# Attention keys turned once, with the two components of a head side by side, and spread over the partitions by the copies out of PSUM

## The chip, the cores and the metric

The kernel runs on one core of one Trainium2 chip, in one launch. The metric is device time in microseconds (us), the median of the runs of a kernel. The engines have these names: PE (TensorE; PEld is its weight load), DVE (VectorE), ACT (ScalarE), POOL (GpSimd) and SP (SyncE, which issues DMAs here).

## The reference

One layer of a hybrid diffusion step: a feed-forward half step, a token mixer, and a second feed-forward half step, on 512 latent tokens and 128 context tokens (640 in all) of width 1024. The mixer runs differential attention, an mLSTM scan in both directions and gates side by side. The change touches the attention, and of that the keys:

```python
def diff_attention(q, k, v, lam):
    ...
        s = jnp.einsum('bqhcd,bkhcd->bhcqk', qi.astype(jnp.float32), kf) * scale
        pr = jax.nn.softmax(s, axis=-1)
        w = pr[:, :, 0] - lam * pr[:, :, 1]
        return jnp.einsum('bhqk,bkhv->bqhv', w, vf)
```

There are 8 heads; `c` is one of two components of 64 features. Each component has scores of its own, and the second softmax is subtracted from the first. Latent queries see the 512 latent keys and 256 cached context keys; context queries see the 128 context keys. The result of each head is normalised over its 128 features.

## The kernel before, in words

**Products.** A product of fp32 numbers is made of rounded parts: each operand is split into a high part (the value rounded to the PE's fp32r format) and a low part (what the rounding left), and the products high x high, low x high and high x low are added in PSUM.

**Scores.** PE contracts over the partitions, so queries and keys of a component must lie with their features on the partitions, and a component has only 64. The kernel uses all 128: for the queries, `qT` holds in component `c` the high part on one half of the partitions and the low part on the other. For the keys, `kH[:, c, :]` holds the high part of component `c` *twice*, once on each half of the partitions, and `kL[:, c, :]` the low part twice. One matmul `qT` with `kH` then gives high x high and low x high at once, one with `kL` gives the rest. `kH` and `kL` are tiles of [128, 2, 896]: for each component the columns 0 to 511 are latent keys, 512 to 767 the cached ones, 768 to 895 the context keys.

**Where the duplicates come from, before.** `k_tok` holds the normalised keys of a pair of heads with tokens on the partitions. `pack_keys` (L1561) writes the high part of a head's keys to `kpk` [128, 5, 4, 64], each component twice side by side, with two ACT copies; `queries` (L1578) writes the low part to `kp2` (named `kp` in the profile) in the same way, with two DVE subtractions. `turn_features` (L1568) then transposes on PE, per token tile of 128 and component, a block of 128 x 128 (one component, doubled): 5 x 2 transposes into three PSUM tiles `ps_qkT` of two, two and one token tiles. Each PSUM tile goes out with one copy over all 128 partitions: to `kH` by DVE (L1593), to `kL` by ACT (L1595; ACT's operations all stand under its helper's line, L51). The same function turns the packed queries.

**Order of the work.** Eight heads follow one another (loop at L1961). Within a head there are five query tiles: `scores`, `soft` (exponentials on ACT), `mix` and the scaling on DVE, `turn` (PE transposes of the weights, `ps_wT`), `values` (`ps_o`). PE does other work between these steps: units of the mixer's projections (`Fill`, L1245), matmuls `ps_t<-wH,hH` and the like, for which ACT rounds a weight block to `wH` and DVE makes `wL`. The table `UNITS` (L1954) says how many units stand where. At the change from one head to the next the loop does `queries` of the next head, a unit, `values(4)` and `finish_norm` of the old head. Behind an even head there follow `keys(0)` (turns `kpk` to `kH`), one unit, `keys(1)` (turns `kp2` to `kL`) and one unit; behind an odd head, five units, with `keys(0)` and `keys(1)` behind the first and the second. Then the next head's `scores(0)` begins. `finish_norm` (L1658) scales the old head's result `ao` on DVE; `finish` (L1667) transposes it on PE (`ps_aT`), behind the unit that follows the next head's `scores(0)`.

PE's instructions keep the order of the program. The orders of ACT, DVE and SP are chosen by a tile scheduler at build time, except inside blocks marked `written()`; each engine then works through its own list in order. The PSUM tiles `ps_qkT`, `ps_t`, `ps_wT`, `ps_o` and `ps_aT` share a pool of five buffers; the scores `sc` have one tile of three banks.

Of the kernel before, what the change touches and what calls it, by code (L numbers as in the profile page):

```python
# [7 lines left out]
F32 = mybir.dt.float32  # L8
F32R = mybir.dt.float32r
BF16 = mybir.dt.bfloat16  # L10
AF = mybir.ActivationFunctionType
ALU = mybir.AluOpType
# [19 lines left out]
def tile_trunk(ctx: ExitStack, tc: tile.TileContext, a: dict):  # L32
    nc = tc.nc
    vec = nc.vector
    as_written = [False]

    def placed(ins):
        if as_written[0] is in_row:
            i = ins.ins
            if i.engine in in_row:  # L40
                tc.add_manual_dep(
                    i, in_row[i.engine].name, mybir.DependencyInfo(mybir.DependencyClass.NoSync, mybir.DependencyReason.DATA),
                    reason="written",
                )
            in_row[i.engine] = i
        elif as_written[0]:
            tc.keep_in_program_order(ins)
        return ins

    def act(*args, **kw):  # L50
        return placed(nc.scalar.activation(*args, **kw))  # L51

    def tt(eng, out, in0, in1, op):
        return placed(eng.tensor_tensor(out=out, in0=in0, in1=in1, op=op))  # L54
# [22 lines left out]
    def tr(*args, **kw):  # L77
        tc.keep_in_program_order(nc.tensor.transpose(*args, **kw))  # L78
# [23 lines left out]
    def load(pool, shape, src, **kw):  # L102
        t = pool.tile(shape, F32, **kw)
        dma(t, src)
        return t
# [725 lines left out]
    with ExitStack() as ph:  # L831
        fp = ph.enter_context(tc.tile_pool(name="ffn1", bufs=1))
        psum = Banks(ph.enter_context(tc.tile_pool(name="ps1", bufs=1, space=PSUM)))
# [507 lines left out]
    identr = gq_p.tile([128, 128], F32R, name="identr")  # L1341
# [7 lines left out]
    psum = att.enter_context(tc.tile_pool(name="ps2", bufs=5, space=PSUM))  # L1349
# [193 lines left out]
    class Head:  # L1543
# [17 lines left out]
        def pack_keys(self):  # L1561
            hs = slice(self.h * 128, (self.h + 1) * 128)
            kv = self.kv = k_tok[self.pr][:, :, hs].rearrange("p t (c d) -> p t c d", c=2)
            self.kpk = ap.tile([128, 5, 4, 64], F32R, tag="pk", name="kpk", bufs=2)
            for i in range(2):
                self.at_act = act(self.kpk[:, :, i::2, :], kv, AF.Copy)

        def turn_features(self, pk, dst, key, ev):  # L1568
            for i0, n in ((0, 2), (2, 2), (4, 1)):
                p = psum.tile([128, 2, 2, 128], F32R, tag="mm", name="ps_qkT")  # L1570
                for i in range(n):
                    flat = pk[:, i0 + i].rearrange("p s d -> p (s d)")
                    for c in range(2):
                        tr(p[:, c, i, :], flat[:, 128 * c : 128 * c + 128], identr)
                o = 768 if key and i0 == 4 else i0 * 128
                ev(dst[:, :, o : o + n * 128].rearrange("p c (i t) -> p c i t", i=n), p[:, :, :n, :].bitcast(F32))

        def queries(self):  # L1578
            self.qT = ap.tile([128, 2, T], F32R, tag="qT", name="qT")
            self.kH = ap.tile([128, 2, 896], F32R, tag="kH", name="kH")  # L1580
            self.kL = ap.tile([128, 2, 896], F32R, tag="kL", name="kL")
            self.ao = ap.tile([128, 5, 128], F32, tag="ao", name="ao")
            self.turn_features(self.qpk, self.qT, False, lambda o, i: act(o, i, AF.Copy))
            self.kp2 = ap.tile([128, 5, 4, 64], F32R, tag="pk", name="kp2", bufs=2)
            for i in range(2):
                self.at_vec = tt(vec, self.kp2[:, :, i::2, :], self.kv, self.kpk[:, :, i::2, :].bitcast(F32), ALU.subtract)
            ck = load(ap, [128, 2, 256], a["cache_kd"][:, self.hd], tag="asq", name="ck")
            act(self.kH[:, :, 512:768], ck, AF.Copy)
            tt(vec, self.kL[:, :, 512:768], ck, self.kH[:, :, 512:768].bitcast(F32), ALU.subtract)

        def keys(self, part):
            if part == 0:
                self.turn_features(self.kpk, self.kH, True, lambda o, i: vec.tensor_copy(o, i))  # L1593
            else:
                self.turn_features(self.kp2, self.kL, True, lambda o, i: act(o, i, AF.Copy))  # L1595

        def scores(self, qi):
            s = ps_s.tile([128, 1536], F32, tag="sc", name="sc")
# [325 lines left out]
    ap = att.enter_context(tc.tile_pool(name="att", bufs=1, reuse_waits="tile"))  # L1924
# [36 lines left out]
    for hd in range(8):  # L1961
        H = heads[hd]
        odd = hd % 2
        for qi in range(5):
            n = UNITS[hd][qi]
# [26 lines left out]
        n = UNITS[hd][-1]  # L1992
# [40 lines left out]
    psum = ml.enter_context(tc.tile_pool(name="ps3", bufs=8, space=PSUM, reuse_waits="tile"))  # L2033
# [238 lines left out]
    psum = Banks(ctx.enter_context(tc.tile_pool(name="ps4", bufs=1, space=PSUM, reuse_waits="tile")))  # L2272
# [58 lines left out]
    t = [in_pools["q"].tile([128, 1024], F32R, tag=f"q{i}", name="wo") for i in range(4)]  # L2331
# [234 lines left out]
```

## Time and profile before

| | |
|---|---|
| runs | 1815.12, 1815.26, 1816.54 us; median 1815.26 |
| the profiled execution | 1815.7 us, of which its span is 1813.9 |
| granted PE clock | 0.999 (mean over the span) |
| key transposes on PE | 160 (80 of `kpk`, 80 of `kp`), 670.5 to 1029.9 us |
| copies of keys out of PSUM | 24 on DVE (`kH`), 24 on ACT (`kL`) |
| attention heads, 655 to 1070 us | PE busy 409.85 of 415.00 us, DVE 273.37, ACT 229.28 |

The profile is of one execution. Rows of the time order read: start, length (us), engine, line, operation, out<-in, form of the tiles, count, and in brackets how long the engine was idle before it and what it was then released by. Matmuls are pipelined, so two may overlap in these rows and the distance from one start to the next is what one costs. Rows of a tile's groups read: operation, tiles, count: shortest/median/longest ns, first and last start, forms.

### The profile page before, as it was taken

Reading aid. Unit: us, or ns where it says so; the run is one execution under the profiler, and the core shown is the slowest. Engines: PE = TensorE matmul, PEld = TensorE weight load, DVE = VectorE, ACT = ScalarE, POOL = GpSimd, SP = SyncE. Lnnn points to the kernel's source line nnn. Section 1 sums busy time; section 2 is a strip of 40 time slices with the busy share of each in tenths; the row PEclk is TensorE's granted clock in tenths of the full one; section 3 lists DMA queues with packets and bytes.
Section 4 is the critical chain, followed back from the end, with each engine's and each line's share of the span. In section 5 each row is a group of like instructions: output and inputs, shape, how many; then the busy total and the mean of one; then the engine's idle time right before and its main releaser. Section 6 shows DMA issues by size and latency. Waiting matters only on the chain.

```text
span 1813.9 us, 30780 instructions
## 1 busy us (share of the span) xinstructions
PE 1785.6 (98%) x12550; PEld 1744.6 (96%) x12550; DVE 1349.6 (74%) x2178; ACT 910.8 (50%) x1588; POOL 39.2 (2%) x69
## 2 busy tenths in 40 slices
PE   8999999999999999999999999999999999999998
PEld 6999999999999999999999998899999999999998
DVE  6879987677888765858584557977767888897485
ACT  5654544333655445556564547674336545554432
POOL 0000000100000000000000000000000000000010
PEclk9999999999999999999999999999999999999999
DMA  8355566977245434221221124576642355557992
GB/s 326 111 198 171 186 236 221 350 227 266 83 139 181 160 131 143 78 69 63 69 69 55 68 81 163 182 257 218 221 171 80 134 173 185 203 180 274 353 311 80
DMA packets 132207, 311.36 MB, mean 172 GB/s; under 512 B 10017, under 2 KB 93217, under 8 KB 119009
## 3 DMA queue, kind: packets, MB, share of 16 engines
q1 hardware_dynamic: 121122, 265.22, 42.3%
q0 software_dynamic: 10256, 41.55, 7.1%
q8 instruction: 98, 1.61, 0.4%
q10 hardware_dynamic: 688, 2.63, 0.4%
q14 instruction: 43, 0.35, 0.1%
HBM read 240.49 MB, written 68.87 MB: 171 GB/s over the span
## 4 chain that ended last, share of the span: by engine, by line
PE 85%; DVE 7%; DMA 4%; ACT 2%; issue 1%; SPq 0%; DVEq 0%; ACTq 0%
PE ps_f L75 48%; PE ps_p L75 14%; PE ps_t L75 12%; PE sc L75 2%; PE ps_n L75 2%; PE ps_o L75 2%; DVE ww L54 2%; PE ps_u L75 1%; DMA raw_a<-in_w_ada_k 1%; PE ps_wT L78 1%; PE ps_qkT L78 1%; DMA raw<-in_w2b 1%; DVE junk L814 1%; DMA P<-nm_dram 1%; DVE mn L1617 1%
## 5 line engine op out<-in xcount | busy, mean ns | idle before, releaser
L75 PE MATMUL ps_f<-S,ww 128*128 128x320 f32 x2400 | 387.5, 310 | 5.2 <-DVE ww L54 1.9
L75 PEld LDWEIGHTS ps_f<-S,ww 128*128 128x128 f32 x2400 | 359.8, 188 | 9.6 <-DVE ww L54 6.5
L54 DVE TENSOR_TENSOR ww<-raw,ww 128x2048 fp32r<-128x2048 f32 (+1 forms) x73 | 163.9, 2246 | 74.3 <-ACT ww L51 74.2
L75 PE MATMUL ps_t<-wH,hH 128*128 128x256 f32 x640 | 185.7, 290 | 0.9 <-DVE x L57 0.9
L75 PE MATMUL ps_f<-hm,ww 128*128 128x320 f32 x1176 | 185.8, 309 | 0.1
L75 PE MATMUL ps_t<-wH,hL 128*128 128x256 f32 x640 | 181.6, 284 | 0.9 <-DVE hL L54 0.9
L75 PE MATMUL ps_t<-wL,hH 128*128 128x256 f32 x640 | 181.4, 283 | 0.0
L75 PEld LDWEIGHTS ps_f<-hm,ww 128*128 128x128 f32 x1176 | 175.7, 188 | 0.6 <-DVE ww L54 0.6
L51 ACT ACTIVATE ww<-raw 128x2048 fp32r<-128x2048 f32 (+1 forms) x73 | 136.9, 1875 | 60.3 <-DVE raw L54 33.0
L54 DVE TENSOR_TENSOR raw<-raw 128x1024 f32<-128x1024 f32 x186 | 161.0, 865 | 2.2
L75 PE MATMUL ps_f<-hm,wB 128*128 128x320 f32 x1008 | 161.5, 309 | 0.0
L75 PE MATMUL ps_p<-hH,wH 128*128 128x320 f32 x480 | 151.1, 315 | 0.7 <-ACT aT L51 0.7
L75 PEld LDWEIGHTS ps_f<-hm,wB 128*128 128x128 f32 x1008 | 151.3, 188 | 0.0
L75 PE MATMUL ps_p<-hH,wL 128*128 128x320 f32 x480 | 148.3, 309 | 0.0
L75 PE MATMUL ps_p<-hL,wH 128*128 128x320 f32 x480 | 148.3, 309 | 0.0
L51 ACT ACTIVATE u<-ps_f 128x320 f32<-128x320 f32 x129 | 55.8, 433 | 161.5 <-PE ps_f L75 159.7
L75 PEld LDWEIGHTS ps_t<-wH,hH 128*128 128x128 f32 x640 | 123.0, 192 | 1.5 <-ACT nsq L51 1.1
L75 PEld LDWEIGHTS ps_t<-wH,hL 128*128 128x128 f32 x640 | 122.9, 192 | 1.1 <-DVE hL L54 1.1
L75 PEld LDWEIGHTS ps_t<-wL,hH 128*128 128x128 f32 x640 | 123.1, 192 | 0.4
L1617 DVE TENSOR_REDUCE mn<-sc 128x2 f32<-128x1536 f32 (+1 forms) x40 | 59.5, 1489 | 56.0 <-PE sc L75 55.8
L54 DVE TENSOR_TENSOR wB<-raw,wB 128x1024 fp32r<-128x1024 f32 x64 | 78.1, 1221 | 26.7 <-ACT wB L51 26.7
L51 ACT ACTIVATE wH<-raw 128x2048 fp32r<-128x2048 f32 (+1 forms) x45 | 75.4, 1681 | 42.2 <-PE ps_p L75 35.5
(309 smaller groups left out, 3621.9 us busy)
## 6 DMA issues: line engine op xcount, KB each, us to landing
g_dram<-g SPq DMA_DIRECT2D x44, 640.0 KB, 7.6
raw_a<-in_w_ada_c POOLq DMA_DIRECT2D x35, 512.0 KB, 4.7
g_dram<-g SPq DMA_DIRECT2D x24, 480.0 KB, 8.1
raw<-in_w1b SPq DMA_DIRECT2D x11, 1024.0 KB, 4.9
raw<-in_w3b SPq DMA_DIRECT2D x11, 1024.0 KB, 6.3
raw<-in_w1a SPq DMA_DIRECT2D x10, 1024.0 KB, 4.9
raw<-in_w3a SPq DMA_DIRECT2D x10, 1024.0 KB, 6.2
hm<-g_dram SPq DMA_DIRECT2D x7, 1280.0 KB, 12.5
```

Source lines behind the costliest of these rows:

```text
L51: return placed(nc.scalar.activation(*args, **kw))
L54: return placed(eng.tensor_tensor(out=out, in0=in0, in1=in1, op=op))
L75: tc.keep_in_program_order(nc.tensor.matmul(*args, **kw))
L78: tc.keep_in_program_order(nc.tensor.transpose(*args, **kw))
L814: placed(vec.tensor_tensor_reduce(out=junk, in0=raw, in1=self.csil[:, v, :], op0=ALU.mult, op1=ALU.add, scale=1.0, scalar=0.0, accum_out=m ...
L1617: placed(vec.tensor_reduce(out=mn, in_=sv, axis=AX.X, op=ALU.min))
```

## The change

Keys are packed once: `kpk` and `kp2` are [128, 5, 2, 64], the two components side by side, with one ACT copy and one DVE subtraction. `turn_features` becomes two functions. `turn_queries` does for the queries what it did. `turn_keys` transposes each token tile once (component 0 comes to lie on partitions 0 to 63, component 1 on 64 to 127): five transposes into two PSUM tiles, of four and one token tiles. Out of PSUM each component is copied twice: by DVE to the partitions it lies on, by ACT to the other half, for `kH` and `kL` alike. These copies have 64 partitions and 512 or 128 columns.

```diff
-            self.kpk = ap.tile([128, 5, 4, 64], F32R, tag="pk", name="kpk", bufs=2)
-            for i in range(2):
-                self.at_act = act(self.kpk[:, :, i::2, :], kv, AF.Copy)
+            self.kpk = ap.tile([128, 5, 2, 64], F32R, tag="pk", name="kpk", bufs=2)
+            self.at_act = act(self.kpk, kv, AF.Copy)
...
+        def turn_keys(self, pk, dst):
+            for i0, n, o in ((0, 4, 0), (4, 1, 768)):
+                p = psum.tile([128, 4, 128], F32R, tag="mm", name="ps_qkT")
+                for i in range(n):
+                    tr(p[:, i, :], pk[:, i0 + i].rearrange("p c d -> p (c d)"), identr)
+                v = p.rearrange("p i t -> p (i t)")[:, : n * 128].bitcast(F32)
+                for c in range(2):
+                    own, other = slice(64 * c, 64 * c + 64), slice(64 - 64 * c, 128 - 64 * c)
+                    vec.tensor_copy(dst[own, c, o : o + n * 128], v[own])
+                    act(dst[other, c, o : o + n * 128], v[own], AF.Copy)
...
-            self.kp2 = ap.tile([128, 5, 4, 64], F32R, tag="pk", name="kp2", bufs=2)
-            for i in range(2):
-                self.at_vec = tt(vec, self.kp2[:, :, i::2, :], self.kv, self.kpk[:, :, i::2, :].bitcast(F32), ALU.subtract)
+            self.turn_queries()
+            self.kp2 = ap.tile([128, 5, 2, 64], F32R, tag="pk", name="kp2", bufs=2)
+            self.at_vec = tt(vec, self.kp2, self.kv, self.kpk.bitcast(F32), ALU.subtract)
...
-            if part == 0:
-                self.turn_features(self.kpk, self.kH, True, lambda o, i: vec.tensor_copy(o, i))
-            else:
-                self.turn_features(self.kp2, self.kL, True, lambda o, i: act(o, i, AF.Copy))
+            self.turn_keys(*((self.kpk, self.kH), (self.kp2, self.kL))[part])
```

PE's order is the same but for the transposes that are gone. The scheduler's orders of DVE and ACT change. Lines behind the edit are 7 higher in the changed kernel (`mn`, L1617 before, is L1624).

DVE between head 0 and head 1, before, from the last copies of `kH` to the first reduction over the scores of head 1 (`ass`, `rv`, `rt`, `ry`: small steps of norms; `ss`: sums of squares for the next pair of heads):

```order
L1593 CAST kH<-ps_qkT 128x2x128 [waits PE_49]
L1663 TENSOR_REDUCE ass<-asq 128x5 [waits Activation_49]
L63 TENSOR_SCALAR rv<-ass 128x5 [waits DVE_49]
L57 SCALAR_TENSOR_TENSOR rt<-ry 128x5 [waits Activation_49]
L54 TENSOR_TENSOR rt<-rt,rv 128x5 [waits DVE_49]
L57 SCALAR_TENSOR_TENSOR ry<-rt,ry 128x5 [waits DVE_49]
L54 TENSOR_TENSOR ao<-ao,ry 128x640 [waits DVE_49]
L54 TENSOR_TENSOR wL<-raw,wH 128x2048 [waits DMAHW5_49,PE_49,Activation_49]
L1475 TENSOR_REDUCE ss<-rope 128x20 [waits DMAHW4_49,DMAHW3_49,DMAHW6_49,DMAHW2_49,DMAHW7_49,DMAHW1_49,Activation_49]
L1617 TENSOR_REDUCE mn<-sc 128x2 [waits PE_49]
```

And in the changed kernel, from the first copies of `kL` on:

```order
L1586 CAST kL<-ps_qkT 64x512 [waits PE_49]
L1586 CAST kL<-ps_qkT 64x128 [waits PE_49]
L54 TENSOR_TENSOR wL<-raw,wH 128x2048 [waits DMAHW5_49,Activation_49]
L1475 TENSOR_REDUCE ss<-rope 128x20 [waits DMAHW4_49,DMAHW3_49,DMAHW6_49,DMAHW2_49,DMAHW7_49,DMAHW1_49,Activation_49]
L57 SCALAR_TENSOR_TENSOR rt<-ry 128x5 [waits Activation_49]
L1586 CAST kL<-ps_qkT 64x512 [waits Activation_49]
L1586 CAST kL<-ps_qkT 64x128 [waits Activation_49]
L63 TENSOR_SCALAR rv<-ss 128x20 [waits DVE_49]
L54 TENSOR_TENSOR rt<-rt,rv 128x5 [waits DVE_49]
L57 SCALAR_TENSOR_TENSOR ry<-rt,ry 128x5 [waits DVE_49]
L54 TENSOR_TENSOR ao<-ao,ry 128x640 [waits DVE_49]
```

The copies of component 0 stand ahead of `wL` and `ss`, those of component 1 (the second 64x512 and 64x128) behind them; each of these waits for ACT, whose copy of component 0 reads the same bank. `ao` stands behind `wL` and `ss` now.

DVE between head 2 and head 3, before, around the row that normalises `ao` and the reduction `mn` over head 3's first scores:

```order
L54 TENSOR_TENSOR rt<-rt,rv 128x5 [waits DVE_49]
L54 TENSOR_TENSOR k_tok<-k_tok,ry 128x1280 [waits DVE_49]
L57 SCALAR_TENSOR_TENSOR ry<-rt,ry 128x5 [waits DVE_49]
L54 TENSOR_TENSOR k_tok<-k_tok,g_kn 128x256 [waits DVE_49]
L54 TENSOR_TENSOR ao<-ao,ry 128x640 [waits DVE_49]
L1617 TENSOR_REDUCE mn<-sc 128x2 [waits PE_49]
L54 TENSOR_TENSOR rope<-rope,ropeBk 128x1024 [waits Activation_49]
L54 TENSOR_TENSOR k_tok<-k_tok,ropeAk 128x1024
```

And in the changed kernel (it reads the same between head 4 and head 5):

```order
L54 TENSOR_TENSOR k_tok<-k_tok,ry 128x1280 [waits DVE_49]
L54 TENSOR_TENSOR rt<-rt,rv 128x5 [waits DVE_49]
L1624 TENSOR_REDUCE mn<-sc 128x2 [waits PE_49]
L54 TENSOR_TENSOR k_tok<-k_tok,g_kn 128x256 [waits DVE_49]
L57 SCALAR_TENSOR_TENSOR ry<-rt,ry 128x5 [waits DVE_49]
L54 TENSOR_TENSOR rope<-rope,ropeBk 128x1024 [waits Activation_49]
L54 TENSOR_TENSOR k_tok<-k_tok,ropeAk 128x1024
L54 TENSOR_TENSOR ao<-ao,ry 128x640 [waits DVE_49]
```

`ao` was ahead of `mn`; it is behind `mn` and the two products with the rope tables.

DVE in head 0, in the changed kernel, around the last copies of `kL` (`Ml`, `fg`, `e`, `b` are the mLSTM's gates):

```order
L54 TENSOR_TENSOR mn<-Ml,bl 64x5 [waits DVE_49]
L54 TENSOR_TENSOR e<-u,Ml 64x640
L1586 CAST kL<-ps_qkT 64x512 [waits Activation_49]
L54 TENSOR_TENSOR b<-fg,b 64x640 [waits DVE_49]
L1586 CAST kL<-ps_qkT 64x128 [waits Activation_49]
```

Before, `e` and `b` stood next to each other there, and DVE had no copy of `kL`.

More of the change, by code (lines that the diff above doesn't have):

```diff
@@ L1563, in pack_keys, with turn_queries @@
             kv = self.kv = k_tok[self.pr][:, :, hs].rearrange("p t (c d) -> p t c d", c=2)
-            self.kpk = ap.tile([128, 5, 4, 64], F32R, tag="pk", name="kpk", bufs=2)
-            for i in range(2):
-                self.at_act = act(self.kpk[:, :, i::2, :], kv, AF.Copy)
-        def turn_features(self, pk, dst, key, ev):
+            self.kpk = ap.tile([128, 5, 2, 64], F32R, tag="pk", name="kpk", bufs=2)
+            self.at_act = act(self.kpk, kv, AF.Copy)
+        def turn_queries(self):
             for i0, n in ((0, 2), (2, 2), (4, 1)):
@@ L1571, in turn_features @@
                 for i in range(n):
-                    flat = pk[:, i0 + i].rearrange("p s d -> p (s d)")
+                    flat = self.qpk[:, i0 + i].rearrange("p s d -> p (s d)")
                     for c in range(2):
                         tr(p[:, c, i, :], flat[:, 128 * c : 128 * c + 128], identr)
-                o = 768 if key and i0 == 4 else i0 * 128
-                ev(dst[:, :, o : o + n * 128].rearrange("p c (i t) -> p c i t", i=n), p[:, :, :n, :].bitcast(F32))
+                o = slice(i0 * 128, (i0 + n) * 128)
+                act(self.qT[:, :, o].rearrange("p c (i t) -> p c i t", i=n), p[:, :, :n, :].bitcast(F32), AF.Copy)
+        def turn_keys(self, pk, dst):
[8 more added lines that the diff above has]
+                    act(dst[other, c, o : o + n * 128], v[own], AF.Copy)
         def queries(self):
@@ L1582, in queries @@
             self.ao = ap.tile([128, 5, 128], F32, tag="ao", name="ao")
-            self.turn_features(self.qpk, self.qT, False, lambda o, i: act(o, i, AF.Copy))
-            self.kp2 = ap.tile([128, 5, 4, 64], F32R, tag="pk", name="kp2", bufs=2)
-            for i in range(2):
-                self.at_vec = tt(vec, self.kp2[:, :, i::2, :], self.kv, self.kpk[:, :, i::2, :].bitcast(F32), ALU.subtract)
+            self.turn_queries()
+            self.kp2 = ap.tile([128, 5, 2, 64], F32R, tag="pk", name="kp2", bufs=2)
+            self.at_vec = tt(vec, self.kp2, self.kv, self.kpk.bitcast(F32), ALU.subtract)
             ck = load(ap, [128, 2, 256], a["cache_kd"][:, self.hd], tag="asq", name="ck")
```

## The prediction

> **What bounds the kernel now.** I read the page's busy times first, then the chain that ended last, then PE's waits in the stretch that holds the attention heads, then the groups of the tiles that the change touches, and last the order of time around the places where the order of DVE changes.
>
> From the page: the engines' busy times, and the chain by engine.
>
> ```profile
> span 1813.9 us, 30780 instructions
> PE 1785.6 (98%) x12550; PEld 1744.6 (96%) x12550; DVE 1349.6 (74%) x2178; ACT 910.8 (50%) x1588; POOL 39.2 (2%) x69
> PE 85%; DVE 7%; DMA 4%; ACT 2%; issue 1%; SPq 0%; DVEq 0%; ACTq 0%
> ```
>
> PE is busy for 98% of the span: what it no longer does is won, and each microsecond that it waits is lost. DVE has a quarter of the span free, ACT half, so their work is dear only where PE waits for one particular result. The answer on waits, PE alone, from 640 to 1080 us, names every wait that it lists there (total us, times, longest):
>
> ```profile
> PE ps_wT L78 <- DVE p L57: 3.0, 7, 0.8
> PE sc L75 <- ACT p L51: 1.6, 3, 0.9
> PE ps_p L75 <- ACT aT L51: 0.7, 1, 0.7
> PE ps_o L75 <- ACT wT L51: 0.5, 1, 0.5
> ```
>
> 5.8 us in all, none of them for a key copy or for the normalised `ao`. The way to read the change is therefore: PE's saving, less the waits that it makes.
>
> **The change part by part.** The groups of its tiles (ns least/median/most, first and last start, forms), and one group of key transposes in the order of time with the matmul behind it:
>
> ```profile
> L78 PE MATMUL ps_qkT<-identr,kpk x80: 222/251/305, 670.5 to 1025.5; 128*128 128x128 f32 x80
> L78 PE MATMUL ps_qkT<-identr,kp x80: 223/251/278, 677.1 to 1029.9; 128*128 128x128 f32 x80
> L1593 DVE CAST kH<-ps_qkT x24: 414/680/692, 673.8 to 1026.5; 128x512 fp32r<-128x512 f32 x16, 128x256 fp32r<-128x256 f32 x8
> L51 ACT ACTIVATE kL<-ps_qkT x24: 387/594/606, 677.6 to 1030.7; 128x512 fp32r<-128x512 f32 x16, 128x256 fp32r<-128x256 f32 x8
> L51 ACT ACTIVATE kpk<-k_tok x16: 720/732/742, 652.9 to 1013.5; 128x640 fp32r<-128x640 f32 x16
> L54 DVE TENSOR_TENSOR kp<-k_tok,kpk x16: 816/820/827, 664.9 to 1021.9; 128x640 fp32r<-128x640 f32 x16
> 781.33 0.97 PE L78 MATMUL ps_qkT<-identr,kpk 128*128 128x128 f32 x10
> 782.14 0.35 PE L75 MATMUL ps_t<-wH,hH 128*128 128x256 f32 x1
> ```
>
> *Transposes (removed).* A group of ten holds PE from 781.33 to 782.14, 0.81 us; I take 0.085 us for one, as the matmuls overlap (251 ns each, but a pitch of a third). 160 become 80: 10 x 0.085 = **0.85 us less per head, 6.8 us in eight heads**. This is on the path.
>
> *Pack and subtract (removed).* One ACT copy of 732 ns and one DVE subtraction of 820 ns less per head. Nothing on PE waits for either now, so alone they bring nothing; they pay for the copies.
>
> *Copies out of PSUM (added).* Three of them in a row on DVE:
>
> ```profile
> 728.25 1.62 DVE L1593 CAST kH<-ps_qkT 128x512 fp32r<-128x512 f32 x3
> ```
>
> They take 1.62 us together, less than 680 + 680 + 414 ns: one of 512 columns starts 0.60 us behind another (1.62 less the last one's 0.414, by two), and I give one of 128 columns a pitch of 0.20. Per head, kH took DVE 680 + 680 + 414 ns and kL took ACT 594 + 594 + 387. Now each of the two engines makes eight copies per head on 64 partitions, four of 512 columns and four of 128. No row has these shapes, so the price needs bounds. One end: a copy on 64 partitions costs what it costs on 128 (680 ns for 512 columns; 128 columns by the line through 680 and 414 ns come to 0.28 us). The other end: half of that. The nearest row is an operation on 64 partitions, beside the 820 ns of the 128-partition subtraction above, both of 640 columns:
>
> ```profile
> 683.06 0.81 DVE L54 TENSOR_TENSOR e<-u,Ml 64x640 f32<-64x640 f32 x1
> 683.79 0.81 DVE L54 TENSOR_TENSOR b<-fg,b 64x640 f32<-64x640 f32 x1
> ```
>
> Half the partitions takes the same time, so I take the full price: on DVE 4 x 0.68 + 4 x 0.28 - 1.77 - 0.82 = +1.25 us per head, and on ACT 4 x 0.59 + 4 x 0.28 - 1.57 - 0.73 = +1.2 us. With a quarter and a half of their span free this is no bound. What counts is the order: the copies of one bank take turns (DVE component 0, ACT component 0, DVE component 1, ACT component 1), so each `kL` bank is complete only after four copies in a row on two queues with other work in them, where before one queue held it.
>
> [...] No row of this trace shows two engines on one bank. [...]
>
> *Place 1, from head 0 to head 1.* In the new order DVE has, behind the copies of component 0 of `kL`, the low part of a weight (`wL`, 2.29 us) and the sum of squares `ss` of the next pair, and only then component 1. Before:
>
> ```profile
> 733.77 1.08 ACT L51 ACTIVATE kL<-ps_qkT 128x512 fp32r<-128x512 f32 x2
> 733.91 2.29 DVE L54 TENSOR_TENSOR wL<-raw,wH 128x2048 fp32r<-128x2048 f32 x1 [1.17 <-ACT wH L51]
> 735.25 0.40 PE L75 MATMUL sc<-kH,qT 128*128 128x512 f32 x1
> 736.06 0.28 PE L75 MATMUL sc<-kL,qT 128*128 128x256 f32 x1
> 736.12 1.48 DVE L1475 TENSOR_REDUCE ss<-rope 128x20 f32<-128x1280 f32 x1
> 736.64 0.28 PE L75 MATMUL ps_t<-wH,hH 128*128 128x256 f32 x1
> 737.51 1.75 DVE L1617 TENSOR_REDUCE mn<-sc 128x2 f32<-128x1536 f32 x1
> ```
>
> `wL` waits for ACT (1.17 us idle), so it and `ss` stay where they are and DVE is free at 737.51. A small operation (0.2) stands ahead of the copy, which runs from 737.7 to 738.4; ACT's copy follows to 739.0. The first score matmul that reads component 1 of `kL` stood at 736.06; it now starts at 739.05, and the unit behind the scores, 0.58 us later as before, at 739.6 instead of 736.64: **+3.0 us**, with the 0.85 saved already inside. Queued behind the waiting matmul is everything of PE; DVE goes on to `ao` and waits for the scores with `mn`.
>
> *Place 2, from head 2 to 3 and from head 4 to 5.* The row of DVE that normalises `ao` stood ahead of `mn`; now it stands behind `mn` and two products with the rope tables, and PE transposes `ao` behind the first unit after the scores. Before, at head 3:
>
> ```profile
> 834.44 0.18 DVE L57 SCALAR_TENSOR_TENSOR rt<-ry 128x20 f32<-128x20 f32 x1 [1.00 <-ACT ry L51]
> 835.09 1.49 DVE L54 TENSOR_TENSOR k_tok<-k_tok,ry 128x1280 f32<-128x1280 f32 x1
> 836.61 0.42 DVE L54 TENSOR_TENSOR k_tok<-k_tok,g_kn 128x256 f32<-128x256 f32 x1
> 836.96 0.82 DVE L54 TENSOR_TENSOR ao<-ao,ry 128x640 f32<-128x640 f32 x1
> 837.36 0.28 PE L75 MATMUL ps_t<-wH,hH 128*128 128x256 f32 x1
> 837.69 1.75 DVE L1617 TENSOR_REDUCE mn<-sc 128x2 f32<-128x1536 f32 x1
> 839.36 1.22 DVE L54 TENSOR_TENSOR rope<-rope,ropeBk 128x1024 f32<-128x1024 f32 x1
> 840.23 0.71 PE L78 MATMUL ps_aT<-ident,ao 128*128 128x128 f32 x5
> 840.49 1.22 DVE L54 TENSOR_TENSOR k_tok<-k_tok,ropeAk 128x1024 f32<-128x1024 f32 x1
> ```
>
> Now: DVE's longer copies (four of 0.60 and four of 0.20 less 1.6, +1.6 by pitch) are met by the missing subtraction (-0.74) and by the idle 1.00, so `k_tok` x `ry` starts as before, about 835.15. By the pitch of the rows (1.41, 0.2, 1.67, 0.46, 1.13, 1.14, each with the start of the next) it, the small `rt`, `mn`, the gain with the small `ry`, and the two rope products end at 841.15, and `ao` ends at 841.97. PE, 0.85 us early, comes to the transposes at 839.4: it waits 2.6 us, net **+1.8 us**. Head 5's order is the same and its rows stand alike, 94 us later: **+1.8** again. By full durations instead of pitches it would be +2.7 each.
>
> *Place 3, head 0.* DVE makes its copies between the gates' operations. Before:
>
> ```profile
> 683.77 0.40 PE L75 MATMUL sc<-kH,qT 128*128 128x512 f32 x1
> 684.58 0.28 PE L75 MATMUL sc<-kL,qT 128*128 128x256 f32 x1
> 685.16 0.28 PE L75 MATMUL ps_t<-wH,hH 128*128 128x256 f32 x1
> ```
>
> In the new order component 1 of `kL` comes between `e` and `b`, and `b` began at 683.79. Up to and with that copy DVE has 4 x 0.60 + 3 x 0.20 = 3.0 us of copies where 1.6 to 1.7 stood, so it ends at 685.1 and ACT's behind it at 685.8. PE's matmul of 684.58 starts there, and the unit at 686.4 instead of 685.16: **+1.2**, and +1.7 by full durations.
>
> *The other heads.* Heads 2, 4 and 7 get no new wait: odd handovers have three units between keys and scores. Each brings -0.85; head 6 about -0.6, for a wait of 0.25. The cover is a unit of projections, 2.9 us (837.36 to 840.23); without it a copy chain of four turns, 2 x 0.68 + 2 x 0.59 = 2.5 us, would stand bare.
>
> *Sum:* 1.2 + 3.0 + 1.8 + 1.8 - 3 x 0.85 - 0.6 = **+4.7 us**; by full durations 1.7 + 3.0 + 2.7 + 2.7 - 3.15 = +7.0. The profiled run took 1815.7 us (span 1813.9 and 1.8 around it), 0.4 above the median of 1815.26; so 1820.4 beside the profiled run and **1820.0** as a median.
>
> **The rivals.** *A wash:* the waits of heads 0 and 1 come, those for `ao` don't, because DVE runs further ahead than the pitches say: 1.2 + 3.0 - 5 x 0.85 - 0.6 = -0.65, 1814.6 us. For it: the idle second ahead of `rt`; against it: 2.6 us would have to go in each.
> *Cheap copies:* 64 partitions cost half. Then place 3 costs nothing (-0.1), place 1 +2.35, place 2 +1.4 each: -0.1 + 2.35 + 2.8 - 2.55 - 0.6 = +1.9, 1817.2 us. Against it are the two 64x640 rows.
> *The other side, faster:* the transposes decide. If each of the four waits stays under a unit's cover, PE just does 80 transposes less: -6.8 us, 1808.5. It decides from the point where the gross waits (2.1 + 3.9 + 2.6 + 2.6 = 11.2) fall under 6.8 in all. For it is PE at 98%; against it, the order puts 3.8 us of `wL` and `ss` before a copy that PE needs.
> *It doesn't do what it says:* excluded for the transposes, which the order shows halved.
>
> **How the numbers follow.** Forecast 0.58 (0.55 of it slower, 0.03 the same), wash 0.20 (0.01 faster, 0.19 same), cheap copies 0.12 (0.10 same, 0.02 slower), full gain 0.08, and 0.02 for longer waits than I counted. A measurement of this kernel can tell about 0.2%, 3.6 us, from no change, so slower begins at 1818.9 us and faster ends at 1811.6. Faster 0.09, same 0.32, slower 0.59. The likeliest case alone spans 1818.2 (one of the two `ao` waits missing, -1.8) to 1822.3 (full durations). The range goes from the wash, with a quarter of a microsecond for the spread of its runs, 1814.3, to 1823.5, full durations with one more wait of a place-3 size, and leaves out the full gain.
>
> **What would show it.** Right, if PE waits in the new profile for ACT `kL` ahead of `sc` in heads 0 and 1 (about 2 and 4 us) and for DVE `ao` ahead of `ps_aT` at heads 2 and 4 (about 2.6 each), with PE's busy time some 7 us lower and the 64x512 copies at about 0.68 and 0.59 us. It is wrong if these waits are under a microsecond, if the copies cost half, if waits elsewhere than at these four places grow by more than 2 us, or if the stretch behind attention, which the change doesn't touch, moves by more than 1 us.

## The result, and the profile after

The changed kernel takes 1825.85 us (median of 6 runs, 1823.74 to 1830.18) beside 1815.19 for the kernel before (6 runs, 1813.88 to 1816.54): a ratio of 1.0063, 95% interval 1.0053 to 1.0074. It is slower, as forecast, but by 10.7 us where 4.7 were forecast, and outside the range. The profiled execution took 1824.75 us, with a span of 1822.9.

The page's busy times and the chain by engine, after:

```profile
span 1822.9 us, 30699 instructions
PE 1783.2 (98%) x12470; PEld 1740.5 (95%) x12470; DVE 1360.5 (75%) x2210; ACT 921.0 (51%) x1620; POOL 39.4 (2%) x69
PE 79%; DVE 11%; DMA 5%; ACT 3%; issue 1%; SPq 1%; DVEq 0%; ACTq 0%
```

80 transposes are gone (12550 - 12470), and 6.8 us of busy time should have gone with them; PE's busy time fell by 2.4 only. Something made PE's other work longer. The waits of PE from 640 to 1090 us, after:

```profile
PE ps_aT L78 <- DVE rc L1638: 5.5, 2, 2.7
PE sc L75 <- ACT kL L51: 5.2, 3, 2.4
PE ps_wT L78 <- DVE p L57: 2.9, 6, 0.8
PE sc L75 <- ACT p L51: 1.6, 3, 0.9
PE ps_o L75 <- ACT wT L51: 0.5, 1, 0.5
```

The two rows on top are new, and they are the forecast's four waits: `ps_aT` twice (the row names `rc`, the small instruction right behind `ao` on DVE), and `sc` for `kL` once in head 0 and twice in head 1. The others are as before, but for the wait of `ps_p` for `aT`, 0.7 us, which is gone. At place 1, from head 0 to head 1, DVE's rows in the order of time read now:

```profile
731.42 0.88 DVE L1586 CAST kL<-ps_qkT 64x512 fp32r<-64x512 f32 x2 [0.43 <-PE ps_qkT L78]
733.70 2.29 DVE L54 TENSOR_TENSOR wL<-raw,wH 128x2048 fp32r<-128x2048 f32 x1 [1.40 <-ACT wH L51]
735.91 1.48 DVE L1475 TENSOR_REDUCE ss<-rope 128x20 f32<-128x1280 f32 x1
737.31 0.16 DVE L57 SCALAR_TENSOR_TENSOR rt<-ry 128x5 f32<-128x5 f32 x1
737.50 0.90 DVE L1586 CAST kL<-ps_qkT 64x512 fp32r<-64x512 f32 x2
```

Component 1 of `kL` stands behind `wL` and `ss`, at 737.50. ACT idles until DVE has copied, and PE until ACT has; ACT's row and PE's rows there:

```profile
738.23 0.76 ACT L51 ACTIVATE kL<-ps_qkT 64x512 fp32r<-64x512 f32 x2 [2.11 <-DVE kL L1586]
735.59 0.50 PE L75 MATMUL sc<-kL,qT 128*128 128x512 f32 x1 [0.96 <-ACT kL L51]
736.17 0.28 PE L75 MATMUL sc<-kH,qT 128*128 128x256 f32 x1
738.87 0.58 PE L75 MATMUL sc<-kL,qT 128*128 128x256 f32 x1 [2.42 <-ACT kL L51]
739.25 0.63 PE L75 MATMUL sc<-kH,qT 128*128 128x512 f32 x1
```

Two waits, 0.96 and 2.42 us. And a thing that was not forecast: the matmuls behind the wait are longer than those ahead of it (0.58 where one of 256 columns took 0.28, 0.63 where one of 512 took 0.40). The answer by windows shows why; its columns are the length, the busy times of PE, PEld, DVE, ACT and POOL, then the granted clock of PE and the DMA's share and rate. The windows begin and end where the clock changes, or a whole number of 3.413 us from there (the length is worked out below the rows):

```profile
735.03:738.44 3.41, 0.86 (x4) 0.60 (x4) 3.35 (x6) 1.27 (x4) 0.00 (x0) 1.00 0.38 86
738.44:741.86 3.42, 2.99 (x12) 2.79 (x13) 2.83 (x6) 0.88 (x4) 0.00 (x0) 0.50 0.52 220
741.86:745.27 3.41, 3.41 (x31) 3.41 (x31) 3.19 (x8) 3.13 (x7) 0.00 (x0) 1.00 0.00 0
...
840.84:844.25 3.41, 2.32 (x20) 2.11 (x18) 3.41 (x5) 2.60 (x6) 0.00 (x0) 1.00 0.11 38
844.25:847.67 3.42, 1.78 (x16) 1.81 (x17) 3.38 (x6) 1.21 (x3) 0.00 (x0) 1.00 0.00 0
...
939.83:943.24 3.41, 1.26 (x11) 1.29 (x12) 3.38 (x7) 1.37 (x5) 0.00 (x0) 1.00 0.06 20
943.24:946.66 3.42, 3.42 (x18) 3.42 (x17) 0.97 (x1) 0.35 (x2) 0.00 (x0) 0.50 0.25 96
```

Behind a window of 3.41 us in which PE was busy for 0.86 us only, the granted clock is 0.50 for just 3.42 us, and then 1.00 again. The same stands behind the wait for `ao` of head 5 (939.83: busy 1.26). Behind that of head 3, as long (2.73 us), it does not: there the wait lies across the border of two windows (busy 2.32 and 1.78), and leaves PE idle for 1.09 us of the one and 1.64 of the other. 943.24 lies 204.80 us behind 738.44, which is 60 times 3.413 us, and the third half-clock stretch of this trace, at 1127.56 behind attention, lies 184.32 us, 54 times 3.413, behind the second: in this trace the stretches start on a grid with steps of 3.413 us. The kernel before has one such stretch in attention, behind a window that was there to be read ahead of the prediction, and was not:

```profile
957.07:960.48 3.41, 1.73 (x13) 1.34 (x13) 2.01 (x6) 3.41 (x8) 0.00 (x0) 1.00 0.12 38
960.48:963.88 3.40, 3.40 (x18) 3.40 (x17) 2.27 (x6) 2.06 (x7) 0.00 (x0) 0.50 0.00 0
```

PE idles 1.68 us in that window, and not in one wait: it waits 0.90 us for `p` ahead of `sc` and 0.78 ahead of `ps_wT`, and the window's idle time is the sum. Here two short waits in one window stand ahead of a half-clock stretch, as one long wait does at 735.03.

**Where the time went.** I laid each matmul group of the one trace beside the same group of the other. Up to 655 us, ahead of everything that the change touches, the changed kernel's profiled execution was 1.7 us ahead (the runs differ there). At 1083 us, behind attention, it was 4.7 us late: attention lost 6.4 us. At 1260 it was 9.3 late, and it stayed so to the end: the stage behind attention lost another 4.5, up to 1.7 of them in the half clock at 1127 (half of 3.41 us, if PE has work for all of it).

### The profile page after: what moved, and what is told of

Read it like the earlier page. It is cut to its first block, busy times and chain, and to the rows that moved or that the text cites. A ratio compares the mean times of both kernels' runs of the same rounds, so it can differ in the third digit from the quotient of the medians.

```text
span 1822.9 us, 30699 instructions
## 1 busy us (share of the span) xinstructions
PE 1783.2 (98%) x12470; PEld 1740.5 (95%) x12470; DVE 1360.5 (75%) x2210; ACT 921.0 (51%) x1620; POOL 39.4 (2%) x69
## 4 chain that ended last, share of the span: by engine, by line
PE 79%; DVE 11%; DMA 5%; ACT 3%; issue 1%; SPq 1%; DVEq 0%; ACTq 0%
PE ps_f L75 46%; PE ps_p L75 14%; PE ps_t L75 9%; PE sc L75 2%; DVE ww L54 2%; PE ps_o L75 2%; DMA raw<-in_w2b 2%; PE ps_n L75 1%; DMA raw_a<-in_w_ada_k 1%; PE ps_wT L78 1%; DMA P<-nm_dram 1%; PE ps_u L75 1%; DVE junk L814 1%; DVE wL L54 1%; DVE mn L1624 1%
## 5 line engine op out<-in xcount | busy, mean ns | idle before, releaser
L1624 DVE TENSOR_REDUCE mn<-sc 128x2 f32<-128x1536 f32 (+1 forms) x40 | 59.6, 1489 | 54.5 <-PE sc L75 54.3
```

What stands on the lines that cost most here:

```text
L1624: placed(vec.tensor_reduce(out=mn, in_=sv, axis=AX.X, op=ALU.min))
```

## The experiments

Two theories stood against each other from the start, and a third came from the last sentence above. **A**: PE's saving of 6.8 us less the four waits, which come from the order on DVE, and (new) the half clock behind long waits. **B**: the doubled copies load DVE and ACT, and that makes everything a little longer. **C**: the stage behind attention loses its 4.5 us for a reason of its own. All ratios are to the kernel before on the same chip.

**The changed kernel again** (no edit).

> The changed kernel once more, for a second trace. Theory A (four waits of PE: component 1 of kL in heads 0 and 1, ao in heads 3 and 5; and, new, half the granted clock for some 3.4 us behind some of these waits, about 1.5 us each): the same four waits, 1.8 to 2.8 us each, and again half clock behind one to three of them, not always behind the same ones; 1823 to 1828 us. Theory B (the doubled copies load DVE and ACT, and everything gets a little longer): waits of PE spread over all heads. Theory C (the stage behind attention lost 4.5 us in the first trace for a reason of its own, an order of DMAs): that stage is again 4 to 5 us longer than before, whatever the clock does there.

1826.42 us (1823.17 to 1830.15; ratio 1.0060, 1.0047 to 1.0072; before 1815.63). The waits are the same to the tenth (5.5 and 5.2 us), at the same four places: A and not B. Half clock again behind the waits of head 1 and head 5, and not behind head 3's. But the stage behind attention, without a half-clock stretch, lost only 0.5 us in this trace. **C falls** as it was put, with 4 to 5 us each time. The length of that stage does vary, though: in the other traces of changed versions without a half clock there, it is 0.3 (covered_heads) to 3.4 us (one_engine) longer than in the first trace of before. Why was not tried.

**ao ahead of mn again, everything else as changed.**

```diff
             with written():
                 H.values(4)
-            H.finish_norm()
+                H.finish_norm()
```

> The changed kernel, with finish_norm in the written order, so that ao stands ahead of mn at heads 3 and 5; transposes and copies are as in the changed kernel. Theory A: the two waits of ps_aT for ao (2.7 us each) go, with the half clock behind one of them; at head 1 ao now stands ahead of component 1 of kL, which costs up to 0.8: 5 to 7 us less than the changed kernel, about 1819. Theory B: the copies are all there, so at most 1 us less, 1825. Theory C: the stage behind attention stays as long as in the changed kernel.

1819.53 us (1816.64 to 1822.47; ratio 1.0020, 1.0012 to 1.0029), 6.9 less than the changed kernel in the same comparison, with every copy still in place. PE's two largest waits:

```profile
PE sc L75 <- ACT kL L51: 5.7, 3, 2.9
PE ps_wT L78 <- DVE p L57: 3.0, 7, 0.8
```

The wait of `ps_aT` is gone from the list; that for `kL` is 0.5 longer, since `ao` now stands ahead of it in head 1. A wait of `ps_p` for `aT`, 0.7, is back (before has it too). The waits account for 5.5 - 0.5 - 0.7 = 4.3 us of the 6.9. The runs' mean clock (below) is 0.9964 where the changed kernel's is 0.9958, which gives about another 1. The rest, some 1.6, stays open; the six runs on the other side alone spread over 7.0. In this trace the wait of head 0 has half clock behind it: it is 1.80 us long and lies inside one window. In the changed kernel's first trace the same wait (1.79) lies across a border of the grid, which leaves PE idle for 1.31 us of one window and 0.47 of the next, and has none. The window of ao_early and the next:

```profile
684.07:687.48 3.41, 1.61 (x11) 1.32 (x10) 3.24 (x9) 2.06 (x5) 0.00 (x0) 1.00 0.53 153
687.48:690.90 3.42, 3.42 (x18) 3.42 (x17) 2.76 (x4) 2.20 (x5) 0.00 (x0) 0.50 0.40 142
```

**Each tile's copies on one engine**: as many copies, no turns.

```diff
-                    vec.tensor_copy(dst[own, c, o : o + n * 128], v[own])
-                    act(dst[other, c, o : o + n * 128], v[own], AF.Copy)
+                    for to in (own, other):
+                        if dst is self.kH:
+                            vec.tensor_copy(dst[to, c, o : o + n * 128], v[own])
+                        else:
+                            act(dst[to, c, o : o + n * 128], v[own], AF.Copy)
```

> The changed kernel, but each tile's copies are on one engine: DVE makes both halves of kH, ACT both halves of kL; as many copies of the same sizes, and no turns between engines. In its order DVE has no kL copy, and ao stands behind mn but ahead of the rope products. Theory A: the waits for kL at heads 0 and 1 go (5.2 us and the half clock behind), and those for ao fall to some tenths: the transposes' 6.8 us show, 1808 to 1811. Theory B: the same number of copies costs as before, 1822 to 1826. Theory C: the stage behind attention stays 4 us longer, so 1812 to 1815.

1822.1 us (1819.15 to 1824.34; ratio 1.0033, 1.0021 to 1.0045): missed by 11 us. The waits for `kL` did go, but others came:

```profile
PE ps_aT L78 <- DVE ao L54: 3.8, 2, 1.9
PE sc L75 <- ACT p L51: 3.0, 4, 1.4
PE ps_wT L78 <- DVE p L57: 2.7, 6, 0.8
PE ps_aT L78 <- DVE r L57: 2.0, 1, 2.0
PE ps_o L75 <- ACT wT L51: 0.5, 1, 0.5
PE sc L75 <- ACT kL L51: 0.4, 1, 0.4
```

Of 5.2 us for `kL` 0.4 are left: without turns there is no wait for the keys. I had taken `ao` right behind `mn` to be early enough; it came 1.9 us late at heads 3 and 5, and in head 1, where it now stood behind `wL`, `mn` and `ss`, 2.0 late (the row that names `r`). Behind head 3's, which leaves PE busy for 1.62 us in the window from 842.49, the next window is at 1.00; the mean clock of the five runs is 0.9956.

**The same with ao ahead of mn** (both edits).

> As one_engine, and finish_norm in the written order, so that ao stands ahead of mn at heads 3 and 5. Theory A: all four waits gone, 1808 to 1810, at most 1 us from one_engine. Theory B: 1822 to 1826. Theory C: 1812 to 1815.

1814.34 us (1811.98 to 1816.24; ratio 0.9993, 0.9984 to 1.0001): no difference from before that could be measured. All four waits are gone, as A has it, and 7.8 us with them, but 1808 to 1810 was expected, and that is missed by 4. By the shift of the matmuls attention gains 1.5 us where the transposes give 6.9: about 1.7 are lost in head 0, 0.5 in head 1 and 2 each at heads 3 and 5, and 0.8 of these come back. `sc` waits 3.0 for `p` (1.6 before) and `ps_wT` 4.2 (3.0). What `mn` gives is later there, behind ACT's copies in the one place and behind `ao` in the others; that this is the reason was not tried.

**Work for PE inside the waits.** The matmuls and transposes put in write where a later product starts anew; no result uses them.

```diff
                         mm(o, qT[:, c, qs], kH[:, c, k0:k1], start=True, stop=False)
+                        if qi == 0 and k0 == 0:
+                            for _ in range({(0, 1): 6, (1, 0): 4, (1, 1): 9}.get((self.hd, c), 0)):
+                                mm(s[:, 1024:1536], qT[:, 0, qs], kH[:, 0, 0:512], start=True, stop=True)
                         mm(o, qT[:, c, qs], kL[:, c, k0:k1], start=False, stop=True)
...
                 p = psum.tile([128, 4, 128], F32, tag="mm", name="ps_aT")
+                if i0 == 0 and self.hd in (2, 4):
+                    for _ in range(16):
+                        tr(p[:, 0, :], ident, ident)
```

> The changed kernel with matmuls that no result uses put into its four waits (6 before component 1 of kL in head 0, 4 and 9 before kL in head 1, each of 512 columns, written where a later product starts anew; 16 transposes of the identity before ps_aT of heads 2 and 4): PE is busy for most of each wait, and goes on when it did. The traces so far put half the granted clock, for 3.41 us, behind windows of 3.41 us in which PE idled for 1.7 to 1.9 us or more. Theory A with this clock: the waits stay as long, counted from the end of the work before them, but the half clock behind them goes; 1.5 to 1.7 us each, 2 to 3 of them in a run: 1821 to 1823.5, against 1826 of the changed kernel. Without an effect of the clock: 1826, or more where the fill is too long.

1820.66 us (1819.31 to 1822.31; ratio 1.0033, 1.0022 to 1.0044), 6.0 over the kernel before of the same comparison, where the changed kernel is 10.7 and 10.8 over its own: 4.7 less, by *adding* work. The trace has no half-clock stretch at all, so the place of the grid isn't known in it; around head 1's waits:

```profile
735.00:738.40 3.40, 3.38 (x21) 2.74 (x21) 2.80 (x2) 2.96 (x6) 0.00 (x0) 1.00 0.00 0
738.40:741.80 3.40, 3.03 (x15) 2.25 (x14) 3.24 (x10) 1.09 (x4) 0.00 (x0) 1.00 0.77 270
```

The useful matmuls start as late as in the changed kernel: beside the first trace of before, PE loses 2.9 us ahead of head 3's `ps_aT` in both. Only the clock behind is different. From 655 to 1083 us this trace loses 3.4 us where the changed kernel's lost 6.4 with two half-clock stretches, so one of them costs 1.5 us.

Each run lists its mean granted clock too: 0.9958 over the 12 runs of the changed kernel, 0.9993 over these 7, and 0.9988 over 71 runs of the kernel before. A half-clock stretch of 3.41 us takes 3.41 x 0.5 / 1820 = 0.00094 off that mean, so by estimate the changed kernel had 4.5 of them in a run, this one 0.7, before 1.3. By this estimate the clock cost the changed kernel (4.5 - 1.3) x 1.5 us = **4.8 us**; at 1.7 each, half of 3.41 us, it would be 5.4.

**One copy per tile over all partitions.** The copy writes the same block for both components, so the scores are not the reference's; half the transposes, as changed.

```diff
-                for c in range(2):
-                    ...
+                v = v[:, None, :].to_broadcast([128, 2, n * 128])
+                if dst is self.kH:
+                    vec.tensor_copy(dst[:, :, o : o + n * 128], v)
+                else:
+                    act(dst[:, :, o : o + n * 128], v, AF.Copy)
```

> Half the transposes as in the changed kernel, but one copy per PSUM tile over all 128 partitions, which writes the same block for both components (DVE for kH, ACT for kL, as before); the partitions' spreading is left out, so the scores are not those of the reference. In its order DVE stands as in before, with ao ahead of mn. Theory A: the transposes' 6.8 us show, no wait is added: 1807.5 to 1809.5. Were the transposes hidden by other work on PE or the saving given back elsewhere: 1813 to 1816.

1810.26 us (1807.44 to 1813.42; ratio 0.9972, 0.9961 to 0.9983), 4.4 less than before's 1814.62, where 5 to 7 were expected. Aligned with the first trace, PE gains 0.43 us at every one of the 16 groups, 6.9 in all; one wait came (`ps_aT` for `ao` in head 1, 1.5 us). The saving is real and on the path. About 1 us of it didn't reach the end; in this trace the stage behind attention was 2.1 longer.

**The changed way only where it is covered.**

```diff
+    NEW = (2, 4, 6, 7)
...
-            self.turn_keys(*((self.kpk, self.kH), (self.kp2, self.kL))[part])
+            if self.hd in NEW:
+                self.turn_keys(*((self.kpk, self.kH), (self.kp2, self.kL))[part])
+            else:
+                ...
```

(The dots stand for the lines of before; `pack_keys` and `queries` are split alike.)

> The changed way for heads 2, 4, 6 and 7 alone, the way of before for heads 0, 1, 3 and 5, where the changed kernel had its four waits. In its order ao stands ahead of mn at heads 3 and 5, and wL and ss behind the kH copies at head 1, as in before. Theory A: four heads bring 0.85 each, none adds more than 0.25: 1812 to 1812.6, faster than both. Were the doubled copies to cost something by themselves (theory B): half of the changed kernel's loss, 1820.

1811.57 us (1809.21 to 1814.42; ratio 0.9984, 0.9975 to 0.9992): half a microsecond under the forecast, and faster than both kernels. The list of PE's waits has the rows of before and no other:

```profile
PE ps_wT L78 <- DVE p L57: 2.7, 6, 0.8
PE sc L75 <- ACT p L51: 1.6, 3, 0.9
PE ps_p L75 <- ACT aT L51: 0.9, 1, 0.9
PE ps_o L75 <- ACT wT L51: 0.5, 1, 0.5
```

By the shift of the matmuls attention gains 3.5 us with all the doubled copies of four heads in it, where four times 0.85 is 3.4. So the copies cost nothing by themselves where the handover is covered: **B falls**.

**The kernel before again.**

> The kernel before, once more, for a second trace: waits in the heads as in the first (5.8 us in all), half the clock at another place or not at all, and the stage behind attention within 2 us of the first trace's length.

1814.46 us. The waits of PE in the heads are the same four rows as before, to the tenth. The half clock stands at 35.72 us and not at 960, so a run of before has it by chance as well; the stage from 1083 to 1260 us was within 0.2 us of the first trace's.

**One of the four waits alone, and filled.** Head 1 is added to the covered heads, then the fill of its waits.

```diff
-    NEW = (2, 4, 6, 7)
+    NEW = (1, 2, 4, 6, 7)
```

> covered_heads, with head 1 the changed way as well, in the changed kernel's order at that place (wL and ss ahead of component 1 of kL): one of the four waits alone. Theory A with the clock: the two waits for kL come back there (1.0 and 2.4 us, less the 0.85 of the transposes) and half the clock for one window behind them, sometimes two (1.5 to 1.7 us each): 4 to 5 us over covered_heads, 1815.5 to 1817. Waits without the clock: 2.5 over it, 1814.

> head1_alone with the fill of 4 and 9 matmuls, which no result uses, in its two waits. Theory A with the clock: PE goes on when it did, the half clock goes: 1.5 to 2 us under head1_alone, 2.5 over covered_heads, 1814. Without an effect of the clock: as head1_alone.

1815.93 us (1812.77 to 1818.38; ratio 1.0004, 0.9995 to 1.0013) and 1815.28 (1811.19 to 1822.15; 1.0005, 0.9995 to 1.0015). Head 1 alone costs 3.9 us (0.8 over before, where covered_heads is 3.1 under): the waits (0.96 + 2.43 in its trace, less 0.85) and some clock. The pair's difference, 0.65, is less than either interval is wide: the times neither show nor exclude the clock. The traces do show it, in the same windows of the one and of the other:

```profile
736.69:740.10 3.41, 0.98 (x6) 0.72 (x5) 3.28 (x8) 1.09 (x4) 0.00 (x0) 1.00 0.68 233
740.10:743.50 3.40, 3.40 (x17) 3.35 (x16) 3.30 (x6) 1.28 (x3) 0.00 (x0) 0.50 0.18 75
...
736.69:740.10 3.41, 3.02 (x14) 2.27 (x15) 3.28 (x9) 1.27 (x5) 0.00 (x0) 1.00 0.57 156
740.10:743.50 3.40, 3.40 (x27) 3.30 (x28) 3.30 (x6) 1.06 (x3) 0.00 (x0) 1.00 0.36 152
```

From 655 to 1083 us the filled trace is 1.5 us better, and that is this stretch. The runs' mean clocks differ by 0.0004 only, which is 0.4 of a stretch with a standard error as large, so how often it comes with head 1 alone is open.

**Six heads.** `NEW = (2, 3, 4, 5, 6, 7)`, and `finish_norm` in the written order behind heads 2 and 4.

> The changed way for heads 2 to 7, with ao in the written order behind heads 2 and 4 so that it stands ahead of mn, and the way of before for heads 0 and 1. Theory A: heads 3 and 5 bring 0.85 each, less some 0.3 to 0.5 for a later p in ao_early's trace: 0.6 to 1.2 us under covered_heads, 1810.4 to 1811. If short handovers lose their saving to later results whatever the order: as covered_heads or up to 1 us above it.

1812.41 us (1809.75 to 1815.66; ratio 0.9984, 0.9975 to 0.9993): as covered_heads, within the interval, and not the 1810.4 to 1811 of theory A. At heads 3 and 5 PE loses 0.7 us ahead of `ps_wT`, which waits for a later `p`, and gets 0.3 to 0.4 of it back; that takes a good part of what the transposes give there.

## Why the prediction was wrong

*The transposes.* 0.85 us per head, 6.8 in all: right (0.43 per group in one_wide_copy, by 16). Head 6 brought 0.6, as forecast.

*The copies' price.* Full price for half the partitions: right. The group of DVE's copies after, least, median and most, mixes 512 and 128 columns:

```profile
L1586 DVE CAST kL<-ps_qkT x32: 272/490/696, 680.3 to 1038.4; 64x512 fp32r<-64x512 f32 x16, 64x128 fp32r<-64x128 f32 x16
L51 ACT ACTIVATE kL<-ps_qkT x32: 256/432/597, 681.0 to 1038.8; 64x512 fp32r<-64x512 f32 x16, 64x128 fp32r<-64x128 f32 x16
```

The ends are the two forms: 0.27 and 0.70 us on DVE, 0.26 and 0.60 on ACT, where 0.28 and 0.68, 0.28 and 0.59 were taken. That they are no bound was right too (covered_heads).

*The four waits.* Right in place and cause, and near in length. Place 1: 0.96 + 2.42 = 3.4 us gross, and between the same matmuls of the two traces +2.95 net up to the last wait, forecast 3.0. Place 2, at head 3:

```profile
840.57 1.76 DVE L1624 TENSOR_REDUCE mn<-sc 128x2 f32<-128x1536 f32 x1
842.65 1.22 DVE L54 TENSOR_TENSOR rope<-rope,ropeBk 128x1024 f32<-128x1024 f32 x1
843.79 1.22 DVE L54 TENSOR_TENSOR k_tok<-k_tok,ropeAk 128x1024 f32<-128x1024 f32 x1
844.93 0.82 DVE L54 TENSOR_TENSOR ao<-ao,ry 128x640 f32<-128x640 f32 x1
845.89 0.74 PE L78 MATMUL ps_aT<-ident,ao 128*128 128x128 f32 x5 [2.73 <-DVE rc L1638]
```

`ao` stands behind `mn` and the rope products and ends at 845.75, and PE waits 2.73 us for it; 2.74 at head 5; 2.6 forecast. Place 3: 1.79 gross, 2.1 forecast.

*The sum.* Attention lost 6.4 us in the first trace. Taking out its two half-clock stretches there (1.5 each), and the one that before's trace had there and this one lacked (1.5), leaves 6.4 - 3.0 + 1.5 = 4.9, against +4.7. filled_waits, which has these waits without the half clock, comes to the same: 3.4 + 1.5 = 4.9. As far as waits and transposes go, the sum was right, and in part by luck: net of the transposes and the clock, heads 0, 1, 3 and 5 cost 1.5 + 2.9 + 2.3 + 2.3 = 9.0 where 1.2 + 3.0 + 1.8 + 1.8 = 7.8 were forecast, and late in attention, around 1020 and 1080 us, 1.3 were gained that the forecast didn't have (there before's wait of `ps_p` for `aT`, 0.7, is gone).

*The step that failed* is the price of a wait: "each microsecond that it waits is lost". In the changed kernel's first trace the waits at heads 1 and 5, which left PE busy for 0.86 and 1.26 us of a 3.41 us window, cost their length *and* half the clock for the next window, 1.5 us more as measured in attention and up to 1.7 by estimate (half of 3.41). By the mean clocks the changed kernel has 4.5 such stretches in a run where the kernel before has 1.3: some 4.8 us, as much as the whole forecast. The range left no room for it, because it was made of uncertain waits and prices alone; the clock was read off the page's line of tenths, where a 3.4 us stretch in a slice of 45 us shows as 9. 10.7 measured, less 4.8, less 4.7, leaves 1.2 that I can't place; the stage behind attention alone differed by 4.1 between the two traces of the changed kernel, half-clock stretch included. Two of the signs that the prediction named for itself told of it: PE's busy time fell by 2.4 us and not by some 7, and in the first trace the stage behind attention moved by 4.5, more than the 1 it allowed.

*The rivals.* The wash failed with the two waits for `ao`, which came, and the cheap copies with the copies' durations. The full gain is what the transposes do bring where a handover has cover; in the changed kernel heads 0 and 1, and heads 3 and 5 with their late `ao`, have none.

*The turns.* Nothing here tried an order in which DVE copies component 1 without waiting for ACT's copy of component 0. one_engine shows what no turns at all do for the keys, 0.4 us of wait for `kL` instead of 5.2.

## What to carry to other kernels

Price a new wait of the bounding engine at its length, and then read from the traces what clock was granted behind waits that are there already: here the stretch at 0.50 behind 1.68 us of idle time stood in the trace of before, such a stretch cost 1.5 us as measured, and a range that allows for it would have been wider. Where a change gives more small instructions to an engine whose order a scheduler chooses, read the new order at every handover for what has moved ahead of, or behind, the one result that PE waits for: where the handover had cover the copies cost nothing, and where the order around them kept PE waiting for `ao` and `kL` they brought 10.7 us of waits and the half clock behind these. And a change that pays where there is cover and costs where there is none can be made for the covered places alone: that version (1811.57 us) beats both kernels.

## What the runs showed of the hardware that was not expected

- The granted clock was 0.50 for 3.41 us at a time, and the stretches of a trace start whole multiples of 3.413 us apart (60 and 54 steps in the changed kernel's first trace, 207 from 34.80 to 741.36 in after_again, 277 from 13.59 to 959.08 in covered_heads). Nine traces with such stretches were read window by window: both of before, both of the changed kernel, ao_early, one_wide_copy, covered_heads, head1_alone and six_heads. Up to the last window of the span they have 18 stretches, 17 of one window and one of two (742.10 in ao_early). Of the windows at full clock, all 14 in which PE idled for 1.90 us or more had half clock behind them (1.90 at 1124.15 and 2.55 at 735.03 in the changed kernel's first trace), of the nine with 1.68 to 1.88 four had it (1.68 at 957.07 in before, 1.80 at 684.07 in ao_early) and five had not (1.88 at 1158.53 in ao_early), and with less none had. What decides between 1.68 and 1.88 is open.
- The grid's phase differs from run to run (a stretch's start, counted from the start of the span, modulo 3.413: 1.33 and 1.59 in two traces of before, 1.16 and 0.67 in two of the changed kernel), so a wait of one length has half clock behind it in one place or run and not in another (2.73 us at head 3 without and 2.74 at head 5 with, in both traces of the changed kernel; 1.8 us in head 0 with it in ao_early and without in the changed kernel). In the changed kernel's 12 runs the time goes with the listed clock, 1823.2 to 1825.2 us at 0.997 and 1829.2 to 1830.2 at 0.994, so much of their spread (standard deviation 2.4 us; 1.4 to 1.8 in the three groups of before's runs) is the clock's.
- A copy out of PSUM over 64 partitions takes as long as over 128: 64x512 0.70 us on DVE and 0.60 on ACT, 128x512 0.68 and 0.59.
